# The last step of windowed attention: a sequence's y split one step sooner, y's low parts on GpSimd, and the tail's values ahead of the next gated column

## The chip, the cores and the metric

One core of a Trainium2 chip runs the whole kernel. The metric is the device time of one execution in microseconds (us), lower being better; where several runs are given, their median counts. The engines are TensorE (PE, matmuls; PEld is its weight load), VectorE (DVE), ScalarE (ACT), GpSimd (POOL) and SyncE (SP, which issues most transfers). Each runs its own instructions strictly in order and waits for the others by semaphores.

## The reference

An encoder layer: RMS norm, one input projection, two parallel branches, a gated merge, and a squared-ReLU MLP, for two sequences of 512 tokens and a model width of 1024. The two branches are what the change lies between:

```
y_att = windowed_attention(q, k, v, sink, bias, mask)      # 16 heads of 64, 4 key heads, blocks of 128
y_ssm = s5_branch(u, ...)                                  # ends: y = gelu(scan(u)); y * sigmoid(y @ w_glu + b_glu)
mixed = sigmoid(g_att) * y_att + sigmoid(g_ssm) * y_ssm
x     = x + mixed @ w_out
```

A query block of 128 tokens sees its own key block and the two beside it; a per-head sink logit joins the softmax. All matrices are float32.

## The kernel before, in words

**Precision.** TensorE multiplies in a rounded float32 (`fp32r`). A float32 operand is split: its high part is a cast to `fp32r`, its low part the original minus the high part, again `fp32r`. A product is three matmuls: high by high, low by high, high by low. A split so costs a cast on one engine and a subtraction on another for each 128x512 tile.

**Attention** runs as eight steps `(j, sq)`: four key heads, two sequences each. A step has four query blocks `qb`; a block is a `Unit`, and its work is spread over two passes of the loop. In pass `qb` the current unit computes the scores of its four query heads (`scores`, L1070, into `sps`), adds the bias and finds the maximum (`largest`, L1074, DVE), and takes the exponent (`exp`, L1080, ACT). In the next pass, as `prev`, its probabilities are turned by the identity (`turn`, L1086, four transposes, for each of the two or three key blocks), split into `ph` (L1090, ACT) and `pl` (L1095, DVE), and multiplied with the values (`value`, L1102, into `po`); then ACT copies one half of `po` (`lower_part`, L1106) and DVE adds the other to it (`add`, L1112). When a unit is made, GpSimd copies the sink column into its `p` (L1062). When a step is done, a `Divide` inverts the row sums, sends them round through memory as `fac`, and GpSimd multiplies `ya` by them (`multiply`, L1141) before `mix_scr<-ya` is stored (L1142).

In passes of earlier steps the next step's query projection (L731) lies between these pieces and fills TensorE. The last step, `j = 3, sq = 1` (index 7), has no next one. What fills it is the first column of the gated product `y @ w_glu`: `first_column(k)` (L1204) is six matmuls for one 128-row chunk `k` of y, three for each sequence, summed in two banks over eight chunks, 48 in all. Column 1 follows, dense, as `ahead.multiply` (L769) behind the tail.

**y's split.** Eight chunks `m`, two sequences: sixteen casts (`y_high`, L1189) and sixteen subtractions (`y_low`, L1195 and L1197). All casts are on ACT, both sequences of a chunk as a pair; the subtraction is DVE's for the first sequence and GpSimd's for the second. All lie in the last step, in pass `qb` chunks `2 qb` and `2 qb + 1`. The raw y comes by six transfers on SP (L1184) behind `mix_scr<-ya`; two of the chunks were loaded before the step. The split parts live in two slots of the memory that the normalised input `hT` had used, and which is free once the last projection is done.

**The tail** behind the loop adds what is owed, turns the last unit's probabilities, multiplies its values, and makes column 1's weights ready: their two loads (`c_raw`, L743) are issued at the end of the last pass, then cast (`c_hi`, L747, ACT) and subtracted (`c_lo`, L748, DVE).

The order of the program is written out by hand: what stands earlier in the code is issued earlier on its engine. Transfers are issued by SP in the order of the code.

## Time and profile before

| | |
|---|---|
| three runs | 1461.7, 1463.05, 1465.93 us (median 1463.05) |
| the profiled execution | 1463.26 us, span 1461.5 us, granted clock 0.996 |
| busy in the span | PE 98%, PEld 84%, DVE 75%, ACT 53%, POOL 11% |
| the last step | 635.43 to 664.27 us of the span |
| the tail, to the 31st matmul of column 1 | 664.27 to 675.70 us |

The profile shows one execution. A timeline row gives the start and the length of an instruction (us from the span's start), its engine, its line, the tiles that it writes and reads, its shape, and in brackets how long the engine stood idle before it and what ended that. Matmul rows overlap: the distance between two starts is the time that one takes in a row of them. The windows view gives the busy time of every engine in a stretch.

### The profile page before, as it was taken

The page shows a single profiled execution, that of the slowest core. Times are in us where ns is not written, and L with a number is a line of the kernel's source. Part 1 is how long each engine was busy: PE and PEld are TensorE (multiplying, and loading weights), DVE is VectorE, ACT ScalarE, POOL GpSimd, SP SyncE. Part 2 cuts the span into 40 slices and gives each one's busy share as a digit, 9 for nine tenths or more (in the row PEclk, how much of TensorE's full clock was granted, in tenths as well). Part 3 has the DMA queues.
Part 4 walks back from the last instruction along what each step waited for, and adds up shares of the span by engine and source line. Part 5 has one row for each costly group of instructions (what it writes and reads, how often), then busy time and mean ns, then how long its engine had stood idle before and what let it go on. Part 6 is the DMA issues. An engine that isn't in the chain of part 4 may idle for free.

```text
span 1461.5 us, 21454 instructions
## 1 busy us (share of the span) xinstructions
PE 1436.7 (98%) x7718; PEld 1227.3 (84%) x7718; DVE 1097.0 (75%) x1856; ACT 775.5 (53%) x1398; POOL 168.0 (11%) x250
## 2 busy tenths in 40 slices
PE   7999999999999999999999989999999999999998
PEld 5888888888999999977888868888888888888887
DVE  8799979974536999998954797777776588475653
ACT  5489862133427999896532455455455444333332
POOL 4111120000213444232001000000000000000000
PEclk9999999999999999999999999999999999999999
DMA  8355567259931332358952334444443894454441
GB/s 305 109 172 173 160 203 274 101 173 296 302 95 51 103 107 76 95 170 265 306 182 87 130 110 155 144 153 151 147 151 130 309 352 130 158 187 147 128 130 58
DMA packets 129238, 243.86 MB, mean 167 GB/s; under 512 B 16059, under 2 KB 59323, under 8 KB 129132
## 3 DMA queue, kind: packets, MB, share of 16 engines
q1 hardware_dynamic: 104684, 186.87, 40.4%
q10 hardware_dynamic: 21888, 46.15, 8.4%
q0 software_dynamic: 2560, 9.48, 2.0%
q8 instruction: 61, 1.00, 0.3%
q14 instruction: 45, 0.37, 0.1%
HBM read 173.20 MB, written 81.82 MB: 174 GB/s over the span
## 4 chain that ended last, share of the span: by engine, by line
PE 91%; DVE 3%; DMA 2%; ACT 2%; issue 1%; POOL 1%; SPq 0%; ACTq 0%; DVEq 0%; POOLq 0%
PE bank L115 14%; PE bank L116 14%; PE bank L117 14%; PE acc L141 11%; PE acc L731 9%; PE acc L769 5%; PE acc L115 3%; PE acc L117 3%; PE acc L116 3%; PE po L1102 2%; PE sps L604 2%; PE sps L1070 2%; PE sps L876 2%; PE tps L1086 2%; PE lag L619 1%
## 5 line engine op out<-in xcount | busy, mean ns | idle before, releaser
L116 PE MATMUL bank<-b_lo,a_hi 128*128 128x512 f32 x440 | 171.2, 389 | 0.0
L117 PE MATMUL bank<-b_hi,a_lo 128*128 128x512 f32 x440 | 171.2, 389 | 0.0
L115 PE MATMUL bank<-b_hi,a_hi 128*128 128x512 f32 x440 | 171.2, 389 | 0.0
L731 PE MATMUL acc<-w_hi,hT 128*128 128x256 f32 x768 | 164.9, 291 | 0.0
L141 PE MATMUL acc<-hT,c_hi 128*128 128x512 f32 x512 | 161.2, 394 | 0.0
L1969 ACT CAST a_hi<-d_a 128x1024 fp32r<-128x1024 f32 x55 | 57.9, 1053 | 178.4 <-PE bank L116 175.3
L1970 DVE TENSOR_TENSOR a_lo<-d_a,a_hi 128x1024 fp32r<-128x1024 f32 x55 | 67.4, 1225 | 100.6 <-ACT a_hi L1969 98.5
L731 PEld LDWEIGHTS acc<-w_hi,hT 128*128 128x128 f32 x768 | 126.6, 190 | 1.7
L141 PEld LDWEIGHTS acc<-hT,c_hi 128*128 128x128 f32 x512 | 94.6, 188 | 21.0 <-issue 2.5
L731 PE MATMUL acc<-w_lo,hT 128*128 128x256 f32 x384 | 108.0, 281 | 0.0
L115 PE MATMUL bank<-act,u_hi 128*128 128x512 f32 x256 | 100.7, 393 | 4.7 <-ACT u L1729 4.7
L116 PE MATMUL bank<-act,u_hi 128*128 128x512 f32 x256 | 100.5, 393 | 0.0
L117 PE MATMUL bank<-act,u_lo 128*128 128x512 f32 x256 | 100.3, 392 | 0.0
L141 PE MATMUL acc<-hT,c_lo 128*128 128x512 f32 x256 | 100.3, 392 | 0.0
L117 PEld LDWEIGHTS bank<-b_hi,a_lo 128*128 128x128 f32 x440 | 82.6, 188 | 17.2
L115 PEld LDWEIGHTS bank<-b_hi,a_hi 128*128 128x128 f32 x440 | 82.6, 188 | 17.2
L116 PEld LDWEIGHTS bank<-b_lo,a_hi 128*128 128x128 f32 x440 | 82.6, 188 | 17.1
L1080 ACT ACTIVATE p<-p,nmx 128x257 f32<-128x257 f32 (+1 forms) x128 | 72.0, 564 | 12.9 <-DVE nmx L1074 12.2
L1753 ACT CAST u_hi<-s 128x512 fp32r<-128x512 f32 x64 | 39.9, 623 | 70.1 <-PE bank L116 52.6
L731 PEld LDWEIGHTS acc<-w_lo,hT 128*128 128x128 f32 x384 | 73.0, 190 | 2.5
L1074 DVE CUSTOM_DVE_ANT_0 p<-sps,bias,nsink 128x256 f32<-128x256 f32 (+1 forms) x128 | 69.3, 542 | 3.7 <-PE sps L1070 2.3
L1970 DVE TENSOR_TENSOR b_lo<-k,b_hi 128x1024 fp32r<-128x1024 f32 x55 | 67.1, 1220 | 0.0
(387 smaller groups left out, 3615.6 us busy)
## 6 DMA issues: line engine op xcount, KB each, us to landing
d_a<-a_scr SPq DMA_DIRECT2D x55, 512.0 KB, 3.6
u_raw<-in_w_up_dram SPq DMA_DIRECT2D x32, 512.0 KB, 5.2
a_scr<-t ACTq DMA_DIRECT2D x64, 256.0 KB, 2.1
k<-in_w_down_dram SPq DMA_DIRECT2D x32, 512.0 KB, 5.8
a_scr<-a ACTq DMA_DIRECT2D x48, 256.0 KB, 3.2
c_raw<-in_w_ug_dram SPq DMA_DIRECT2D x44, 256.0 KB, 3.3
ct_scr<-ctab SPq DMA_DIRECT2D x16, 576.0 KB, 3.3
ctab_in<-ct_scr SPq DMA_DIRECT2D x32, 288.0 KB, 4.7
```

The costliest lines, as they stand in the source:

```text
L115: PE.matmul(ps, a[0], b[0], start=first, stop=False)
L116: PE.matmul(ps, a[0], b[1], start=False, stop=False)
L117: PE.matmul(ps, a[1], b[0], start=False, stop=last)
L141: PE.matmul(self.ps[s], self.w[p == 2][:, k, :], hT[s][p == 1][:, k, :], start=i % (3 * KT) == 0, stop=i % (3 * KT) == 3 * KT - 1)
L604: PE.matmul(ps[:, i * P:(i + 1) * P], bm[:, ri, g, :], u_sb[:, g, :], start=True, stop=True)
L731: PE.matmul(ps, act[p == 2][:, k, col:col + P], self.w[k // 4][p == 1][:, k % 4, :], start=i == 0, stop=i == 3 * KT - 1)
L769: PE.matmul(self.ps[s], w_g[self.m][p == 2][:, k, :], y_part(s, int(p == 1), k), start=k + p == 0, stop=k == KT - 1 and p == 2)
L1074: V.tensor_tensor_reduce(self.p[:, h, 1:1 + self.nk], self.s[h][:, 0:self.nk], biases[self.j][h][:, b0:b0 + self.nk], -1.0, nsink[:, hh:hh ...
L1080: S.activation(p, p, AF.Exp, bias=self.nmx[:, h:h + 1], scale=-1.0, accum_out=self.sums[:, h, self.qb:self.qb + 1])
L1753: S.copy(hi, src)
L1969: S.copy(hi, src)
L1970: V.tensor_sub(lo, src, hi.bitcast(F32))
```

## The change

The memory slot for the first sequence's y is opened at the very start, and `hT` of the first sequence lives in it: that `hT` is last read in step 5, so the slot is free for y in step 6. There, in passes 2 and 3, GpSimd casts and subtracts the first sequence's chunks 0 and 1, ahead of `made.multiply`. In the last step ACT makes eight casts instead of sixteen, one at a time (the second sequence's chunks 0 and 1, the first sequence's chunks 2 to 7), DVE six (the second sequence's chunks 2 to 7), and GpSimd all fourteen subtractions. The first two chunks of the first sequence are multiplied in pass 0 right behind the first turn. The gate multiply of step 6's result moves behind the last subtractions. The loads of column 1's weights are issued in the last step right behind y's. In the tail, `first_column(7)` is cut in two around the second turn, the values come ahead of column 1, and column 1's casts and subtractions follow `ph` and `pl`.

```diff
+    slot_a = opers.enter_context(tc.tile_pool(name="slot_a", bufs=1, side="right", reuse_waits="tile"))
-    hT = [[hpool.tile([P, KT, HALF], F32R, name=f"hT{s}_{i}") for i in range(2)] for s in range(NSEQ)]
+    hT = [slot(slot_a), [hpool.tile([P, KT, HALF], F32R, name=f"hT1_{i}") for i in range(2)]]
...
-        def y_high(m, yr):
-            for s in range(NSEQ):
-                S.copy(y_part(s, 0, m).rearrange("p (t k) -> p t k", t=T), yr[:, :, s, :])
-
-        def y_low(m, yr):
-            for s in range(NSEQ):
-                lo, hi = [y_part(s, i, m).rearrange("p (t k) -> p t k", t=T) for i in (1, 0)]
-                if s:
-                    GP.tensor_tensor(lo, yr[:, :, s, :], hi.bitcast(F32), op=ALU.subtract)
-                else:
-                    V.tensor_sub(lo, yr[:, :, s, :], hi.bitcast(F32))
-
-        def first_column(k):
-            for s in range(NSEQ):
+        def y_high(m, s, copy):
+            copy(y_part(s, 0, m).rearrange("p (t k) -> p t k", t=T), y_rows[m][:, :, s, :])
+
+        def y_low(m, s):
+            lo, hi = [y_part(s, i, m).rearrange("p (t k) -> p t k", t=T) for i in (1, 0)]
+            GP.tensor_tensor(lo, y_rows[m][:, :, s, :], hi.bitcast(F32), op=ALU.subtract)
+
+        def first_column(k, seqs=range(NSEQ)):
+            for s in seqs:
...
-                    if i == len(steps) - 1:
-                        y_high(2 * qb, y_rows[2 * qb])
                     cur.scores(1)
...
+                    if last and qb == 1:
+                        w_g[1], parts1 = column_parts(1, False)
+                        for load, part in parts1:
+                            load()
+                    if last and qb:
+                        y_high(2 * qb, 1, V.tensor_copy)
+                        for s in range(NSEQ):
+                            y_low(2 * qb, s)
                     if n3:
                         prev.turn(0)
                         prev.high(0)
+                    if last and not qb:
+                        y_high(0, 1, S.copy)
+                        y_low(0, 1)
                     project(8)
                     if n3:
                         prev.low(0)
-                    if i == len(steps) - 1 and qb:
-                        first_column(2 * qb - 1)
+                    if last:
+                        if qb == 0:
+                            first_column(0, (0,))
+                            first_column(1, (0,))
+                        elif qb == 1:
+                            first_column(1, (1,))
+                        else:
+                            first_column(2 * qb - 1)
...
-                    if made and qb == NB - 1:
+                    if i == len(steps) - 2 and qb >= 2:
+                        y_high(qb - 2, 0, GP.tensor_copy)
+                        y_low(qb - 2, 0)
+                    if made and qb == NB - 1 and not last:
                         made.multiply()
                         made = None
...
-                    if i == len(steps) - 1:
-                        y_low(2 * qb, y_rows[2 * qb])
+                    if last and turned:
+                        turned.low()
+                        turned = None
...
-                    if i == len(steps) - 1:
-                        y_high(2 * qb + 1, y_rows[2 * qb + 1])
+                    if last:
+                        y_high(2 * qb + 1, 0 if qb else 1, S.copy)
...
                     cur.largest(3)
+                    if last:
+                        if qb:
+                            y_high(2 * qb + 1, 1, V.tensor_copy)
+                            y_low(2 * qb + 1, 0)
+                        y_low(2 * qb + 1, 1)
+                        if made and qb == NB - 1:
+                            made.multiply()
+                            made = None
...
-                    if i == len(steps) - 1:
-                        y_low(2 * qb + 1, y_rows[2 * qb + 1])
-                        first_column(2 * qb)
+                    if last:
+                        first_column(2 * qb, range(NSEQ) if qb else (1,))
...
+                    if last and qb < NB - 1:
+                        y_high(2 * qb + 2, 0, S.copy)
                     if n3:
                         prev.lower_part()
...
-                    if i == len(steps) - 1 and qb == NB - 1:
-                        w_g[1], subs_g = column_parts(1)
-                        for sub in subs_g:
-                            sub()
...
-            first_column(KT - 1)
+            first_column(KT - 1, (0,))
             prev.low(0)
             prev.turn(1)
             prev.high(1)
+            first_column(KT - 1, (1,))
+            subs_g = [part() for load, part in parts1]
+            prev.low(1)
+            for sub in subs_g:
+                sub()
+            for n in range(2):
+                for part in range(2):
+                    prev.value(n, part)
+            prev.lower_part()
...
             ahead.multiply(6)
-            prev.value(0, 0)
-            prev.low(1)
+            prev.add()
+            div = Divide(*steps[-1], *done, True)
+            div.invert()
             V.tensor_mul(at0, at0, ga0)
-            prev.value(0, 1)
             ahead.multiply(6)
-            prev.value(1, 0)
+            div.turn()
...
-            ahead.multiply(6)
-            prev.lower_part()
-            prev.add()
-            div = Divide(*steps[-1], *done, True)
-            div.invert()
-            ahead.multiply(12)
-            div.turn()
+            ahead.multiply(18)
             div.multiply()
```

How the instructions stand at three places (the line numbers of the changed kernel are one to a few higher). First TensorE, from the scores that open the last step: `tps<-ident,p` is a turn, `po<-ph,va` a value, and `acc<-act...` the first column. Before:

```order
L1070 MATMUL sps<-kl,qa 128x256
L1086 MATMUL tps<-ident,p 128x128 x4
L1070 MATMUL sps<-kh,qa 128x256
L1070 MATMUL sps<-kl,qa 128x256
L1086 MATMUL tps<-ident,p 128x128 x4
L1102 MATMUL po<-ph,va 128x512
```

and now:

```order
L1071 MATMUL sps<-kl,qa 128x256
L1087 MATMUL tps<-ident,p 128x128 x4
L1200 MATMUL acc<-act_7265,c_hi 128x512
L1200 MATMUL acc<-act_7266,c_hi 128x512
L1200 MATMUL acc<-act_7265,c_lo 128x512
L1200 MATMUL acc<-act_7265,c_hi 128x512
L1200 MATMUL acc<-act_7266,c_hi 128x512
L1200 MATMUL acc<-act_7265,c_lo 128x512
L1071 MATMUL sps<-kh,qa 128x256
L1071 MATMUL sps<-kl,qa 128x256
L1087 MATMUL tps<-ident,p 128x128 x4
L1103 MATMUL po<-ph,va 128x512
```

Six matmuls of the first sequence have come between the first turn and the next scores; before, the first matmul of the column stood behind the second unit of values.

Then ScalarE from the same place (`yr` is a raw chunk of y, `act0` its high part). Before:

```order
L1106 COPY ol_7682<-po_7637 64x512
L1189 CAST act0_7691<-yr_7370 128x512
L1189 CAST act0_7693<-yr_7370 128x512
L1090 CAST ph_7734<-tps_7729 128x512
L1080 ACTIVATE p_7709,sm_7696<-p_7709,nmx_7711 128x257 x2
L1090 CAST ph_7753<-tps_7748 128x512
L1189 CAST act0_7691<-yr_7372 128x512
L1189 CAST act0_7693<-yr_7372 128x512
```

and now:

```order
L1107 COPY ol_7691<-po_7646 64x512
L1091 CAST ph_7736<-tps_7731 128x512
L1189 CAST act0_7697<-yr_7375 128x512
L1081 ACTIVATE p_7713,sm_7700<-p_7713,nmx_7715 128x257 x2
L1091 CAST ph_7764<-tps_7759 128x512
L1189 CAST act0_7697<-yr_7377 128x512
L1081 ACTIVATE p_7713,sm_7700<-p_7713,nmx_7715 128x257
```

The pair of casts that stood ahead of `ph` is gone, and one cast for each chunk stands behind it.

Last GpSimd, from the row statistics of step 6's last pass into the last step (`ya<-ya,fac` is the gate multiply, `p<-nsink` the sink column of a new unit). Before:

```order
L1024 TENSOR_TENSOR rq<-ms,neg_half 128x4
L1141 TENSOR_TENSOR ya<-ya,fac 128x1024
L1062 COPY p<-nsink 128x4
L1023 TENSOR_SCALAR ms<-ms 128x4
L1024 TENSOR_TENSOR rq<-ms,neg_half 128x4
L1195 TENSOR_TENSOR b_7694<-yr,act_7693 128x512 x2
L1062 COPY p<-nsink 128x4
```

and now:

```order
L1025 TENSOR_TENSOR rq<-ms,neg_half 128x4
L1189 CAST act_7265<-yr 128x512
L1193 TENSOR_TENSOR act_7266<-yr,act_7265 128x512
L1142 TENSOR_TENSOR ya<-ya,fac 128x1024
L1063 COPY p<-nsink 128x4
L1024 TENSOR_SCALAR ms<-ms 128x4
L1025 TENSOR_TENSOR rq<-ms,neg_half 128x4
L1193 TENSOR_TENSOR b_7698<-yr,act_7697 128x512 x2
L1063 COPY p<-nsink 128x4
L1193 TENSOR_TENSOR act_7266<-yr,act_7265 128x512
L1193 TENSOR_TENSOR b_7698<-yr,act_7697 128x512
```

A cast and a subtraction of the first sequence have come ahead of the multiply, and from the second pass on each chunk has two subtractions where it had one.

More of the change, by code (lines that the diff above doesn't have):

```diff
@@ L1234, in hybrid_layer @@
                 extra = pieces_of(i)
+                last = i == len(steps) - 1
+                if i == len(steps) - 2:
+                    y_tiles = [[[t_[:, 0:4, :], t_[:, 4:8, :]] for t_ in slot(slot_a)]]
                 if i == len(steps) - 1:
@@ L1357, in hybrid_layer @@
                     hpool_cm.__exit__(None, None, None)
-                    slot_a, slot_b = [opers.enter_context(tc.tile_pool(name=f"slot_{n}", bufs=1, side="right", reuse_waits="tile"))
-                                      for n in "ab"]
-                    y_tiles = [[[t_[:, 0:4, :], t_[:, 4:8, :]] for t_ in slot(slot_a)], split_slot()]
+                    slot_b = opers.enter_context(tc.tile_pool(name="slot_b", bufs=1, side="right", reuse_waits="tile"))
+                    y_tiles.append(split_slot())
             loads_in_order.__exit__(None, None, None)
@@ L1380, in hybrid_layer @@
             ahead.multiply(6)
-            prev.value(0, 0)
-            prev.low(1)
+            prev.add()
+            div = Divide(*steps[-1], *done, True)
+            div.invert()
             V.tensor_mul(at0, at0, ga0)
-            prev.value(0, 1)
             ahead.multiply(6)
-            prev.value(1, 0)
+            div.turn()
             V.tensor_mul(gs0, gs0, y_rows[0])
-            prev.value(1, 1)
             w_g[2], subs_g = column_parts(2)
```

## The prediction

> **What bounds the kernel now.** I read the page's first part, then the stretches of the last attention step, then that stretch's rows engine by engine. On the whole TensorE sets the time:
>
> ```profile
> PE 1436.7 (98%) x7718; PEld 1227.3 (84%) x7718; DVE 1097.0 (75%) x1856; ACT 775.5 (53%) x1398; POOL 168.0 (11%) x250
> ```
>
> So only PE's gaps can be won, and the change touches one place with gaps: the last step (four query blocks, which I call units 0 to 3) and the tail behind it. The windows are those four units, the tail up to the 31st matmul of GLU column 1, and a stretch behind it; columns are length, then busy time and count of PE, PEld, DVE, ACT and POOL:
>
> ```profile
> 635.43:643.41 7.98, 5.75 (x29) 3.87 (x28) 7.14 (x19) 7.16 (x19) 3.91 (x5) 1.00 0.97 351
> 643.41:649.59 6.18, 6.18 (x34) 5.22 (x33) 5.54 (x16) 5.90 (x15) 2.19 (x2) 1.00 0.38 133
> 649.59:657.24 7.65, 7.42 (x40) 5.82 (x38) 7.05 (x17) 7.09 (x18) 3.27 (x5) 1.00 0.83 222
> 657.24:664.27 7.03, 6.87 (x40) 5.43 (x38) 6.41 (x16) 6.28 (x16) 4.96 (x3) 1.00 0.45 145
> 664.27:675.70 11.43, 10.92 (x51) 8.13 (x49) 8.58 (x15) 8.01 (x12) 0.00 (x0) 1.00 0.82 280
> 676.00:690.00 14.00, 14.00 (x63) 11.57 (x62) 13.02 (x16) 7.42 (x12) 1.81 (x3) 1.00 0.95 284
> ```
>
> PE is dense from 676 on, so time won before 675.70 reaches the end undiminished. Idle up to there: 7.98 - 5.75 = 2.23 in unit 0, then 0, 0.23, 0.16 and 0.51: 3.13 us. Clock 1.00 throughout. The gaps by PE's timeline (start, length, in brackets the idle time and what ended it):
>
> ```profile
> 638.30 0.50 PE L1102 MATMUL po<-ph,va 128*128 128x512 f32 x1 [0.94 <-ACT ph L1090]
> ...
> 642.38 0.50 PE L1204 MATMUL acc<-act,c_hi 128*128 128x512 f32 x1 [1.28 <-DVE qa L1050]
> ...
> 644.11 0.60 PE L1086 MATMUL tps<-ident,p 128*128 128x128 f32 x4
> ...
> 657.72 0.60 PE L1086 MATMUL tps<-ident,p 128*128 128x128 f32 x4
> 658.07 0.71 PE L1204 MATMUL acc<-act,c_hi 128*128 128x512 f32 x2
> ...
> 674.31 0.39 PE L769 MATMUL acc<-act,c_hi 128*128 128x512 f32 x1
> ...
> 675.44 0.39 PE L769 MATMUL acc<-act,c_lo 128*128 128x512 f32 x1
> ```
>
> Spacings back to back: a 512-column matmul 0.226 ((675.44 - 674.31)/5); the four scores that open a unit 0.48 at 256 columns (657.72 - 657.24), 0.70 at 384 (644.11 - 643.41); a turn of four transposes 0.35 (658.07 - 657.72). Behind the gap of unit 0 stand ACT's y casts, in the tail GLU column 1's weights, which land late:
>
> ```profile
> 636.50 1.14 ACT L1189 CAST act<-yr 128x512 fp32r<-128x512 f32 x2
> 637.66 0.58 ACT L1090 CAST ph<-tps 128x512 fp32r<-128x512 f32 x1
> ...
> 639.61 1.14 ACT L1189 CAST act<-yr 128x512 fp32r<-128x512 f32 x2
> ...
> 665.79 1.32 ACT L747 CAST c_hi<-c_raw 128x512 fp32r<-128x512 f32 x2 [0.74 <-DMA c_raw<-in_w_glu_dram]
> ```
>
> VectorE's rows of the same stretch: two low parts of y, column 1's subtractions, and the add that frees the value bank.
>
> ```profile
> 639.62 0.69 DVE L1197 TENSOR_TENSOR act<-yr,act 128x512 fp32r<-128x512 f32 x1
> ...
> 660.72 1.38 DVE L1197 TENSOR_TENSOR act<-yr_pair,act 128x512 fp32r<-128x512 f32 x1
> ...
> 666.50 1.33 DVE L748 TENSOR_TENSOR c_lo<-c_raw,c_hi 128x512 fp32r<-128x512 f32 x2 [2.03 <-ACT c_hi L747]
> 667.75 0.84 DVE L1112 TENSOR_TENSOR ya<-po,ol 64x256 f32<-64x256 f32 x2
> ```
>
> **The change, part by part.** PE, ACT and DVE run in order, so I placed the new order unit by unit. "Lead" is how much sooner PE has done the same work.
>
> Unit 0. The two casts ahead of ph go: ph starts 637.66 - 636.50 = 1.16 sooner. Of the pair at 639.61 one stays: 0.57 less ahead of qa, the operand that ended the 1.28 gap. DVE's subtraction at 639.62 goes; its 0.6 was partly covered by qa's wait for ACT, I count half. Together 1.16 + 0.57 + 0.3 = 2.0: unit 1 starts at 641.4 instead of 643.41. Three more column matmuls (first sequence, chunk 1) are done by then, 3 x 0.226 = 0.68. Lead 2.7.
>
> Unit 1 gives back. It was dense before because the gap let ACT and DVE catch up. Now ACT, with 7.16 - 0.57 = 6.6 of work from 635.43, is still 0.65 behind at 641.4. DVE gets a cast ahead of the first pl, and meets POOL. The cast's price is not in the trace: no dense one-source DVE operation of 128x512 with both sides in SBUF exists before. Its bounds:
>
> ```profile
> L337 DVE TENSOR_TENSOR dt<-ex_q,ex_i 128x64 f32<-128x64 f32 x1 | 0.2, 227 | 0.0
> L326 DVE TENSOR_SCALAR ex_n<-ex_r 128x64 f32<-128x64 f32 x2 | 0.4, 196 | 0.1
> L864 DVE COPY st<-h 64x512 f32<-64x512 f32 x32 | 24.3, 767 | 3.6 <-PE sps L876 2.9
> ```
>
> One source saves 0.031 at 64 elements; if that is per element, 0.25 at 512: 0.69 - 0.25 = 0.44, the low end. The high end is the widely strided copy, 0.77. The y cast reads runs of adjacent elements, nearer to the dense rows: I take 0.44. The Trainium skill (VectorE: DVE Perf Modes, § The perf-mode tier table) gives a one-source fp32 copy in SBUF twice the rate of a two-source one, which scaled is an estimate of 0.43; by it the sum is the same, and no row here shows it at this size. While POOL subtracts, a DVE operation waits: the subtraction at 660.72 took 1.38 instead of 0.69 beside the first row here, and the second pair, early in the program, is worse:
>
> ```profile
> 660.25 1.29 POOL L1195 TENSOR_TENSOR b<-yr_pair,act 128x512 fp32r<-128x512 f32 x1
> ```
>
> Of the second pair, VectorE's row and GpSimd's:
>
> ```profile
> 15.37 1.77 DVE L220 TENSOR_TENSOR c_lo<-c_raw,c_hi 128x512 fp32r<-128x512 f32 x1
> ```
>
> ```profile
> 14.98 1.61 POOL L366 TENSOR_TENSOR hT<-rn_xn,hT 128x512 fp32r<-128x512 f32 x1 [3.52 <-ACT hT L364]
> ```
>
> So a blocked operation costs 0.69 to 1.08 more, one that meets nothing 0. By my placing the first cast of a unit comes up late in a POOL subtraction: 0.45. Unit 1 loses 0.65 + 0.44 + 0.45 = 1.5; lead at unit 2: 1.2. Bounds: lead 0 if everything is given back, 2.7 if PE stays dense.
>
> Unit 2: 0.44 + 0.45 less the 0.6 of the subtraction that leaves: loses 0.3, lead 0.9. Unit 3: the same 0.3, 0.3 more because the second cast waits longer (about 0.7), less the 0.69 that 660.72 had waited: gains 0.1. The tail starts 1.0 sooner, at 663.25.
>
> POOL's room: four subtractions and a small copy in each of units 1 to 3, 4 x 1.29 + 0.2 = 5.4 of about 7; in the last also the gate multiply, behind them, whose transfer is not due before the tail is over.
>
> ```profile
> L1062 POOL COPY p<-nsink 128x4 f32<-128x4 f32 x32 | 6.1, 192 | 0.0
> ```
>
> That copy brings in the sink column, which the unit's first exp on ACT reads, and it now stands behind the last subtraction of the unit before. That subtraction needs a DVE cast that follows the unit's last score row: in unit 1 I place it at 648.4, its end at 649.7, the copy's at 649.9 and unit 2's exp at 650.0. Cost nothing, with 0.1 to spare; every further delay on POOL is a delay of exp, up to 1.29 if the subtraction before it is late too. The Trainium skill (GPSIMD Engine Reference, § 4.1) speaks against the move: two-input elementwise work takes about twice as long there as on VectorE. The trace agrees, 1.29 against 0.69; by it the change costs POOL 8 x 1.29 more for 8 x 0.69 saved on DVE, and the sum is unchanged while POOL has room.
>
> Tail. Column 1's weights are now asked for in unit 1 instead of here, so the casts and subtractions at 665.79 and 666.50 no longer wait for a landing; the add (667.75) moves ahead of the subtractions, which frees the bank for the values:
>
> ```profile
> 660.74 1.98 SPq L743 DMA_DIRECT2D c_raw<-in_w_glu_dram  x2
> ```
>
> After 663.25: turn 0.35, three matmuls 0.68, turn 0.35, three matmuls 0.68, to 665.3; the values follow ph and pl (0.58 and 0.69 each, the last pl at about 666.3), and column 1 runs dense from 666.7. Before, 30 back-to-back matmuls ending at 675.70 would start at 675.70 - 30 x 0.226 = 668.9. Lead 2.1.
>
> Step before. Two POOL casts and two subtractions come in ahead. The price of one cast from a copy, then the rows of POOL, of DVE and of PE that the casts meet:
>
> ```profile
> L988 POOL COPY kd<-kn 128x512 f32<-128x512 f32 x8 | 4.9, 610 | 0.0
> ```
>
> ```profile
> 623.42 1.04 POOL L1024 TENSOR_TENSOR rq<-ms,neg_half 128x4 f32<-128x4 f32 x1
> ...
> 631.51 2.41 POOL L1141 TENSOR_TENSOR ya<-ya,fac 128x1024 f32<-128x1024 f32 x1
> ```
>
> ```profile
> 625.81 0.69 DVE L748 TENSOR_TENSOR c_lo<-c_raw,c_hi 128x512 fp32r<-128x512 f32 x1
> ...
> 627.55 0.69 DVE L1095 TENSOR_TENSOR pl<-tps,ph 128x512 fp32r<-128x512 f32 x1
> ```
>
> ```profile
> 628.29 0.50 PE L1102 MATMUL po<-pl,va 128*128 128x512 f32 x1
> ```
>
> The first pair runs 624.4 (623.42 + 1.04) to 626.3 and holds up the subtraction at 625.81: it would end at 626.83 instead of 626.50. DVE has next to no gap from there to the pl at 627.55, whose end at 628.24 is what lets PE's value start at 628.29: -0.33 (0 if the chain has slack, -0.7 as at 660.72). The second pair pushes the multiply, and the stores and loads behind it on SP's queue, by 0.61 + 1.29 = 1.9:
>
> ```profile
> 633.95 0.38 SPq L1142 DMA_DIRECT2D mix_scr<-ya  x1
> 634.42 2.88 SPq L1184 DMA_DIRECT2D yr<-y_scr  x4
> ```
>
> ```profile
> DMA to landing us min/median/max: 5.2/5.7/6.9
> ```
>
> The first load, y block 2, now issues at 636.3 and lands near 641.7 (5.4 later, between the row's least and median); ACT comes to its cast at about 642.0. It is hidden with 0.3 to spare.
>
> Sum: 2.1 - 0.33 = 1.7 us. The profiled execution took 1463.26 with a span of 1461.5 (1.8 around it); the runs' median is 1463.05, 0.2 below. Forecast 1463.05 - 1.7 = 1461.4. A cast of 0.77 takes another 0.33 in each of units 1 to 3, 1.0 in all: 1462.4.
>
> **The rivals.** (B) PE stays bound. Work to 675.70: 102 matmuls (48 of column 0, 24 values, 30 of column 1) x 0.226 = 23.1, scores 0.48 x 4 + 0.70 x 4 = 4.7 (units 0 and 3 have the short ones), 12 turns x 0.35 = 4.2, 0.4 of small transposes: 32.4 of 40.3 us. All idle (3.1) and half of the other 4.8 gone, less 0.33: gain 5.2, 1457.9. For: ACT has eight casts fewer and DVE two operations fewer, and neither is full in the windows. Against: unit 1 was dense only behind 2.23 of idle in unit 0.
>
> (C) Slower: GpSimd's 14 subtractions and DVE's six casts take turns. POOL is busy 5.4 of 7 in units 1 to 3, so a cast meets a running subtraction most times, and each wait is handed on to the sink copy and exp. At 0.69 to 1.08 for each of six instead of the 1.5 that I counted, 4.1 to 6.5: 2.6 to 5.0 more, 3.8 in the middle; a sixth of it I put beside other waits, 3.2 on the path. 1.5 more than the 1.7 gained: 1464.6. It decides once the six casts wait over 1.5 + 1.7 = 3.2 in sum, 0.53 each. The rows above speak for it, most pl and score rows, which read PSUM, at 0.69 and 0.48 to 0.62 against. The Trainium skill (SBUF — State Buffer, § Who interferes with whom) states it as an exclusive lock, the later one blocked for the whole instruction; the trace agrees at 660.72.
>
> (D) The late y loads: block 2 takes the row's longest landing, 6.9 instead of 5.4, and comes at 643.2, 1.2 us after ACT wants it. ACT's casts, the chain behind and unit 1 slip by that: gain 0.5, 1462.5.
>
> (E) No effect: the first stall of unit 0 moves whole to ph and pl in unit 1, and the tail's 1.1 goes to waits of the values and to the step before: 1463.1. For: unit 1's backlog of 0.65. Against: the late landing at 665.79 goes in any case.
>
> **How the numbers follow.** Forecast 0.42, B 0.18, C 0.17, D 0.12, E 0.11. A difference over 0.3% (4.4 us) is what a measurement of this kernel can tell from none. Faster by more needs under 1458.7: two thirds of B, 0.12. Slower by more needs over 1467.4: a fifth of C and 0.03 for what I have not seen, 0.06. Within: 0.82. Range: B's end to C's, 1458.0 to 1465.0.
>
> **What would show it.** Right: PE's 0.94 and 1.28 gaps of unit 0 gone or under half; unit 1 longer than PE's content; DVE casts of 0.4 to 0.5 where POOL rests, 0.9 to 1.2 where not; no wait for c_raw in the tail; dense column 1 about 2 us sooner against the step's start, and the step's own start 0.3 later. Wrong: PE waiting for act parts from POOL, ACT's exp waiting for POOL, ACT waiting for yr, DVE casts of 1.2 and more throughout, or PE idle under 1 us in the whole stretch.

## The result, and the profile after

The changed kernel takes 1456.25 us (median of nine runs, 1454.72 to 1459.61), the kernel before 1463.45 us beside it (nine runs, 1461.7 to 1466.78): a ratio of 0.9950, 95% interval 0.9937 to 0.9963. It is 7.2 us faster; the forecast was 1.7 us, and the time lies below the range. The profiled execution took 1455.62 us with a span of 1453.8.

The change's own stretch came out near the forecast in size. The gain has another source, 180 us behind it, at a place that the prediction does not mention.

**The last step.** The page's busy times after the change, for the whole span:

```profile
PE 1434.8 (99%) x7718; PEld 1227.8 (84%) x7718; DVE 1094.3 (75%) x1854; ACT 770.0 (53%) x1390; POOL 179.3 (12%) x260
```

The windows of the four units, of the tail up to the 31st matmul of column 1, and of two stretches behind it, after the change (length; busy time and count of PE, PEld, DVE, ACT, POOL; granted clock; DMA share; GB/s):

```profile
635.90:641.92 6.02, 5.43 (x32) 4.46 (x31) 5.87 (x17) 5.55 (x15) 4.53 (x7) 1.00 0.74 214
641.92:648.76 6.84, 6.32 (x31) 4.63 (x30) 5.68 (x16) 5.24 (x14) 3.87 (x3) 1.00 1.03 411
648.76:656.69 7.93, 7.57 (x39) 5.84 (x38) 6.57 (x18) 6.89 (x17) 6.17 (x6) 1.00 0.74 231
656.69:663.68 6.99, 6.71 (x40) 5.51 (x39) 5.80 (x15) 4.85 (x13) 5.24 (x6) 1.00 0.23 58
663.68:674.16 10.48, 10.48 (x50) 8.20 (x49) 7.79 (x13) 8.60 (x14) 3.30 (x3) 1.00 0.67 219
674.00:690.00 16.00, 16.00 (x72) 13.15 (x71) 14.97 (x17) 6.54 (x11) 4.55 (x4) 1.00 1.02 354
690.00:703.00 13.00, 11.57 (x52) 9.22 (x51) 11.61 (x15) 5.97 (x10) 0.00 (x0) 1.00 0.90 291
```

Counted from the start of the step, units 1, 2, 3 and the tail begin at 6.02, 12.86, 20.79 and 27.78 us; before, at 7.98, 14.16, 21.81 and 28.84. So the lead is 1.96, 1.30, 1.02 and 1.06, where 2.0, 1.2, 0.9 and 1.0 was forecast. The 31st matmul of column 1 is reached 10.48 behind the tail's start instead of 11.43, a lead of 2.0 (forecast 2.1); with the later start of the step (635.90 against 635.43) 1.54 us are left at 674.16 (forecast 1.7).

The last row but one is dense; the last has 1.43 us of idle, and before it had none. That is the first place where the forecast breaks: the waits of PE between 690 and 712, after the change (the time in all, the count, the longest; before, this stretch has none):

```profile
PE acc L770 <- DVE c_lo L749: 1.4, 1, 1.4
```

The operand that column 4 starts with comes from DVE's subtraction, which starts almost when it did before. The row of the changed kernel, then of the kernel before, by DVE's timeline:

```profile
701.38 1.29 DVE L749 TENSOR_TENSOR c_lo<-c_raw,c_hi 128x512 fp32r<-128x512 f32 x2
```

```profile
701.54 1.28 DVE L748 TENSOR_TENSOR c_lo<-c_raw,c_hi 128x512 fp32r<-128x512 f32 x2
```

Only 0.16 sooner. With the matmuls of the two traces paired by their number, the lead is 1.6 at 670, and 0.12 to 0.16 from 704 to 850. All that the edits won was gone 30 us behind them.

**Where the 7 us come from.** At 851 the output projection ends and the up projection of the MLP begins. Of the kernel before, the waits of PE have this row, the longest of the program behind its first products:

```profile
PE bank L115 <- ACT u L1729: 4.7, 1, 4.7
```

PE's timeline of the kernel before, the last matmul into the old accumulators, the first into the new ones, and the thirteenth:

```profile
851.10 0.39 PE L117 MATMUL acc<-act,f 128*128 128x512 f32 x1
856.23 0.79 PE L115 MATMUL bank<-act,u_hi 128*128 128x512 f32 x1 [4.74 <-ACT u L1729]
...
861.35 0.40 PE L115 MATMUL bank<-act,u_hi 128*128 128x512 f32 x1
```

Its windows of the idle time and of those twelve matmuls:

```profile
851.00:856.20 5.20, 0.49 (x3) 0.07 (x1) 5.11 (x10) 4.52 (x8) 0.00 (x0) 0.82 0.02 9
856.23:861.09 4.86, 4.86 (x12) 3.80 (x12) 4.78 (x8) 3.60 (x6) 0.00 (x0) 0.50 0.17 53
```

PE stands idle for 4.74 us, and then runs at a granted clock of 0.50: twelve matmuls in 5.1 us (856.23 to 861.35), 0.426 each instead of 0.227. After the change the same place reads, by PE's timeline:

```profile
850.94 0.39 PE L117 MATMUL acc<-act,f 128*128 128x512 f32 x1
851.17 0.39 PE L115 MATMUL bank<-act,u_hi 128*128 128x512 f32 x1
```

No wait, and no slow matmuls: 4.74 + 12 x (0.426 - 0.227) = 7.1 us. The paired matmuls show 7.3, a lead of 0.16 at 850 and 7.47 at 863, which stays to the end; the 0.16 between the two is there because the idle time is counted from the end of a row of 0.39, in a stream whose rows start 0.227 apart.

**Why the wait was there.** The front of the program has three accumulators, handed out again as they come free; the up projection opens a new pool of eight over the same memory. Behind 851 ACT still has to copy one old accumulator out, and comes to it late, since its other work is queued ahead (ACT's timeline, before):

```profile
854.56 0.63 ACT L1741 ACTIVATE a<-a 128x512 f32<-128x512 f32 x1
...
855.59 0.59 ACT L1729 COPY u<-acc 128x512 f32<-128x512 f32 x1 [0.40 <-ACT a L1741]
```

In the program's assignment of memory that accumulator lies, before the change, on the same bank (bank 0) as the first of the eight new ones. In the changed kernel `first_column` asks for its first accumulator earlier, ahead of the one that the query turn of the step uses; the two change places, and from there on banks 0 and 2 are swapped for every later accumulator of the front. The one that ACT copies late is then on bank 2, which the up projection needs later.

### The profile page after: what moved, and what is told of

Its sections match the earlier page's. It is cut to its first block, busy times and chain, and to the rows that moved or that the text cites. A ratio compares the mean times of both kernels' runs of the same rounds, so it can differ in the third digit from the quotient of the medians.

```text
span 1453.8 us, 21452 instructions
## 1 busy us (share of the span) xinstructions
PE 1434.8 (99%) x7718; PEld 1227.8 (84%) x7718; DVE 1094.3 (75%) x1854; ACT 770.0 (53%) x1390; POOL 179.3 (12%) x260
## 4 chain that ended last, share of the span: by engine, by line
PE 90%; DVE 4%; DMA 2%; ACT 1%; issue 1%; POOL 0%; SPq 0%; DVEq 0%; ACTq 0%
PE bank L116 14%; PE bank L117 14%; PE bank L115 14%; PE acc L141 11%; PE acc L732 9%; PE acc L115 3%; PE acc L117 3%; PE acc L116 3%; PE acc L770 3%; PE po L1103 2%; PE sps L605 2%; PE sps L1071 2%; PE sps L877 2%; PE tps L1087 2%; PE lag L620 1%
## 5 line engine op out<-in xcount | busy, mean ns | idle before, releaser
L732 PE MATMUL acc<-w_hi,hT 128*128 128x256 f32 x384 | 84.4, 293 | 0.0
L732 PE MATMUL acc<-w_hi,act 128*128 128x256 f32 x384 | 81.2, 290 | 0.0
L141 PE MATMUL acc<-act,c_hi 128*128 128x512 f32 x256 | 80.6, 395 | 0.0
L141 PE MATMUL acc<-hT,c_hi 128*128 128x512 f32 x256 | 80.5, 394 | 0.0
L732 PEld LDWEIGHTS acc<-w_hi,hT 128*128 128x128 f32 x384 | 63.8, 190 | 0.9
L732 PEld LDWEIGHTS acc<-w_hi,act 128*128 128x128 f32 x384 | 63.1, 190 | 0.8
L1993 ACT CAST b_hi<-k 128x1024 fp32r<-128x1024 f32 x55 | 57.7, 1051 | 0.0
```

Of the source, the lines that this page charges most:

```text
L141: PE.matmul(self.ps[s], self.w[p == 2][:, k, :], hT[s][p == 1][:, k, :], start=i % (3 * KT) == 0, stop=i % (3 * KT) == 3 * KT - 1)
L732: PE.matmul(ps, act[p == 2][:, k, col:col + P], self.w[k // 4][p == 1][:, k % 4, :], start=i == 0, stop=i == 3 * KT - 1)
L1993: S.copy(hi, src)
```

## The experiments

Two theories for the gain. **Rotation:** the swap of the accumulators, and nothing else, makes the 7 us; the edits of the last step are worth nothing in the end. **Edits:** the changed last step makes at least a good part of it. For the slow matmuls: the halved clock follows from the idle time. For the lost lead: several causes of the late operand, below.

**1. Only the rotation, in the kernel before.** One dummy transpose takes an accumulator more in the output projection, so that all later ones move on by one place; nothing of the change is in it.

```diff
             add = rows1[t].half(1)
+            if t == 3:
+                PE.transpose(acc()[:, 0:P], ident, ident)
             if t == 3:
```

> The kernel before with one small transpose more (0.1 us) into an accumulator late in the output projection, so that the three accumulators rotate on by one and the first product of the up projection no longer falls on the accumulator that ACT copies as u; attention is untouched. Theory 1 (the measured gain comes from this collision, 180 us behind the change): no 4.7 us wait at the up projection, no spell at half clock behind it, 1463.4 - 7.3 = 1456.1. Theory 2 (the gain comes from the attention step, as the change meant): 1463.4, no change.

Measured: 1456.12 us, ratio 0.9947 (0.9932 to 0.9961). PE's timeline at the place has no idle time any more:

```profile
850.48 0.39 PE L115 MATMUL bank<-act,u_hi 128*128 128x512 f32 x1
```

One line that computes nothing gives the whole gain of the change.

**2. The collision put back into the changed kernel.** The same line, there.

> The changed kernel with the same small transpose, which there turns the accumulators so that the collision is back; the attention step stays changed. Theory 1: the wait of 4.7 us for ACT's u and the half clock are back, 1456.3 + 7.3 = 1463.6, level with the kernel before. Theory 2: 1456.3, the gain stays.

Measured: 1462.89 us, ratio 0.9996 (0.9988 to 1.0005). PE's timeline and the window of what follows the idle time:

```profile
856.57 0.80 PE L115 MATMUL bank<-act,u_hi 128*128 128x512 f32 x1 [4.74 <-ACT u L1755]
```

```profile
856.57:861.20 4.63, 4.63 (x11) 3.71 (x12) 4.54 (x8) 3.60 (x6) 0.00 (x0) 0.50 0.13 46
```

The wait and the half clock are back, and with them the time of the kernel before. This is also the measure of the edits alone, with the dummy transpose of 0.1: between 1.8 us faster and 0.7 us slower by the interval. Rotation holds, edits falls.

**3. The idle time filled, in the kernel before.** Twenty more matmuls of the same shape into a spare tile keep PE busy until ACT's copy is done; the collision stays.

```diff
     p1 = product(acc(), first[1][0], B11)
     p2 = product(acc(), first[1][1], B21)
+    fill = tps()
+    for _ in range(20):
+        PE.matmul(fill, first[1][1][0][:, 0, :], B21[0][:, 0, :], start=True, stop=True)
```

> The kernel before with 20 extra matmuls of 128x512 (4.5 us, result unused) in the gap ahead of the up projection, so that TensorE does not idle while it waits for ACT's u. Theory A (the twelve slow matmuls at 0.43 us are the price of the idle stretch, through the granted clock): the first product still starts near 856.2, the matmuls behind it take 0.227, 2.4 us less: 1461.0. Rival B (the first products are slow by what they read or by what runs beside them): 1463.4, still 0.43 each.

Measured: 1461.51 us, ratio 0.9985 (0.9976 to 0.9993). PE's timeline, and the window of what follows:

```profile
856.28 0.50 PE L115 MATMUL bank<-act,u_hi 128*128 128x512 f32 x1 [0.22 <-ACT u L1729]
```

```profile
856.30:861.00 4.70, 4.70 (x21) 3.90 (x22) 4.61 (x8) 3.89 (x7) 0.00 (x0) 1.00 0.13 45
```

Full clock, and the up projection starts when it did. So the slow matmuls come from the idle time ahead of them, and not from what runs beside them. 2.4 us were expected of it and 1.6 came; the lead by paired matmuls is 2.2 at 863 and 1.7 at the end, and the 0.5 lost between 1200 and 1300 were not followed.

**4. Half filled:** nine matmuls instead of twenty, one run.

> The kernel before with 9 extra matmuls (2.0 us) at the start of the gap ahead of the up projection, so that 2.7 us of idle are left of 4.9. If any idle of this length halves the granted clock, the twelve slow matmuls stay; if the clock falls only after a longer idle, they run at 0.227 as with 20. I expect the latter, with no rule of this case to say so.

Measured: 1462.23 us (one run; 1463.25 before on the same chip). PE's timeline:

```profile
855.85 0.50 PE L115 MATMUL bank<-act,u_hi 128*128 128x512 f32 x1 [2.70 <-ACT u L1729]
...
856.90 0.54 PE L116 MATMUL bank<-act,u_hi 128*128 128x512 f32 x1
857.24 0.63 PE L117 MATMUL bank<-act,u_lo 128*128 128x512 f32 x1
```

Against what was expected, 2.70 us of idle time also halve the clock, but not at once: behind the first, three matmuls follow at about 0.23, and from 856.90 on they take up to 0.43 until 860.2, some 3.3 us.

The next runs ask why the lead of 1.6 us is lost at column 4.

**5. The subtractions of the next column's weights put ahead of the mixing** in each column of the changed kernel.

```diff
                 gl = bank_out(m, col.ps[s])
-                if not ending:
-                    low = late()
                 for sub in subs:
                     sub()
+                if not ending:
+                    low = late()
```

> The changed kernel with one move in the gated columns: the subtractions that make the next column's low weights stand ahead of the mixing of the column before on VectorE, not behind it. Theory 1 (the attention step did win 1.8 us, and 1.4 of it are lost again where TensorE waits for c_lo at the fourth column): that wait goes, 1456.3 - 1.4 = 1454.9. Rival (VectorE is full there, and what is now late takes the wait's place): 1456.3.

Measured: 1455.59 us, ratio 0.9943 (0.9930 to 0.9955), and the wait for `c_lo` is still 1.4. The time lies between the two answers expected; by the wait, this order in DVE's queue is not what holds the operand: in the trace the gate product ahead of it now waits 1.91 for `ga`, and the subtraction starts at 701.18.

**6. GpSimd's last gate multiply left out**, in the changed kernel; the values that it scales go out unscaled, so a part of the attention's result is missing. It runs from 685.75 and holds up a DVE operation that takes 0.69 elsewhere (DVE's timeline of the changed kernel):

```profile
686.24 2.61 DVE L1580 TENSOR_TENSOR at<-z,at 128x512 f32<-128x512 f32 x1
```

```diff
             ahead.multiply(18)
-            div.multiply()
+            GP.dma_start(mix_scr[6:8, :, HALF:2 * HALF].rearrange("m p t -> p m t"), div.ya)
```

> The changed kernel without GpSimd's last gate multiply (128x1024, 2.4 us; left out, so the last key head's second sequence is stored unscaled). Theory 1 (the 1.4 us lost at the fourth column come from this multiply, which blocks a VectorE operation for 1.9 us at 686 and so delays the gate product, the load of the next gate and at last c_lo): no VectorE row of 2.6, the wait for the gate's load (1.28) gone or small, no wait for c_lo, 1456.2 - 1.4 = 1454.8. Rival (VectorE is paced by the gate's load in any case): c_lo where it was, 1456.2.

Measured: 1455.33 us, ratio 0.9947 (0.9934 to 0.9961); the wait is 0.9. Without the blocked operation the gate products of DVE still stand at 689.98 and 695.83, now waiting for `w_raw` (1.36) and `ga` (0.98). The wait is 0.5 shorter in this one trace, with PE 0.3 later; in the median the difference is no larger than the runs' scatter. What the change did move is where the block falls: GpSimd's multiply ran at 691.52 in the kernel before, behind the gate product of 688.73; now it runs at 685.75, ahead of that product, which stands at 689.98. That this is what costs the lead is not shown, since the product stands there without the multiply too.

**7. The gate product put ahead of the mixing**, so that its buffer comes free, and its next load starts, sooner (changed kernel; `gate_at` is the product of `at` and `ga`, taken out of `gate_in`). The subtractions stand ahead of the mixing too, as in run 5.

```diff
-            V.tensor_mul(at, at, ga)
...
-                if not ending:
-                    low = late()
                 for sub in subs:
                     sub()
...
+                if gate:
+                    gate_at(gate)
+                if not ending:
+                    low = late()
                 if gate:
                     gate_in(gate, low)
```

> The changed kernel with another order on VectorE in the gated columns: first the next column's low weights, then the product with the gate, which frees the gate's buffer, and only then the mixing of the column before. Theory 1 (the gate's load is issued late because its buffer is freed late): the load is issued some 1.5 us sooner at the third column, the idle time of 1.28 goes, c_lo at the fourth column is 1 to 1.5 us sooner and so is all that follows: 1455.0. Rival (the column stage is bound by VectorE's sum of work, the order does nothing): 1456.2.

Measured: 1461.23 us, ratio 0.9984 (0.9975 to 0.9993): 5 us worse than the changed kernel, and neither of the answers expected. The waits of PE, and a window behind them:

```profile
PE acc L770 <- ACT c_hi L748: 2.4, 1, 2.4
PE acc L770 <- DVE c_lo L749: 0.6, 1, 0.6
```

```profile
704.00:708.00 4.00, 3.89 (x9) 3.12 (x10) 3.28 (x6) 1.21 (x2) 0.00 (x0) 0.50 0.85 282
```

DVE waits for `ga` with the mixing queued behind it, ACT's cast comes late in turn, and the idle time of 3.0 us brings the half clock here too.

**8. The tail and the early weights alone**, in the kernel before (one run): column 1's loads in unit 1, the tail in its new order, y's split as it was.

```diff
+                    if i == len(steps) - 1 and qb == 1:
+                        w_g[1], parts1 = column_parts(1, False)
+                        for load, part in parts1:
+                            load()
...
-            first_column(KT - 1)
+            first_column(KT - 1, (0,))
...
+            first_column(KT - 1, (1,))
+            subs_g = [part() for load, part in parts1]
+            prev.low(1)
...
```

> The kernel before with only the tail of the change: column 1's weights loaded behind y, the last values and the last add ahead of column 1; y's split stays as it was. Theory 1 (by my sum the tail is worth 1.1 us, the rest of the 2.2 comes from the moved casts): from the step's start at 635.4 to the 31st matmul of column 1 39.2 us instead of 40.3, then all of it lost at the fourth column; total level with before. Rival (late weights were the whole local gain): 38.0 us.

Measured: 1467.8 us, one run, against 1463.25; level was expected. The waits:

```profile
PE bank L115 <- ACT u L1731: 4.7, 1, 4.7
PE acc L769 <- DVE c_lo L748: 1.8, 1, 1.8
```

From the step's start the 31st matmul of column 1 comes after 39.32 us, as expected (39.2; 40.27 in the trace before). But runs 1 and 4, which leave the last step as it was, reach it after 39.37 and 39.34 (more on this below). This trace begins the step 0.75 later than the one before, so by paired matmuls it leads by only 0.25 at 670; through the wait at column 4 and the slow clock behind it, it is 3.0 behind from 706 on. The collision is still there: the early request for an accumulator in pass 0 belongs to y's split, not to the tail.

**9. The store that SP waits for.** In the changed kernel `mix_scr<-ya` goes out at 666.41, behind the moved gate multiply (664.00 to 666.4), and the loads behind it with it; the DMA engines stand still from 660 to 664. Here that multiply is left out and its store issued earlier (the mixing of that part takes values without their gate).

```diff
+                    if made and qb == NB - 1 and last:
+                        SP.dma_start(mix_scr[2 * made.j:2 * made.j + 2, :, made.sq * HALF:(made.sq + 1) * HALF].rearrange("m p t -> p m t"), made.ya)
+                        made = None
...
-                            made.multiply()
```

> The changed kernel without GpSimd's gate multiply of the seventh result (step 6) in the last step; its store to mix_scr goes out on SP in the same step without it, so the mixing takes an ungated value there (that part of the output is left out). Theory: in the changed kernel the store at 666.41 waits behind that multiply (664.00 to 666.4), and every load behind it on SP with it, so that the DMA engines stand idle until 664 to 668 and the fourth column waits 1.4 us for c_lo. Without the multiply the store is issued before 664, the engines are busy from about 660 on, the wait for c_lo falls under .5, and the end comes 1.0 to 1.6 sooner: 1454.9. Rival: the gate loads are paced by their buffers and by the transfers of the weights, the wait stays over 1.0 and the time is that of the changed kernel, 1456.2.

Measured: 1457.34 us, ratio 0.9958 (0.9945 to 0.9970), beside 1456.48 for the changed kernel itself on the same chip (ratio 0.9959, 0.9946 to 0.9971):

> The changed kernel itself, as the measure for the two others: 1456.2, as in its first runs, with a wait of the fourth column for c_lo of 1.4 us and no wait of the up projection's first product.

The wait for `c_lo` is 1.8, not under 0.5. SP's queue without the multiply, then with it:

```profile
656.93 0.32 SPq L1560 DMA_DIRECT2D gs<-gs_scr  x1
666.93 0.94 SPq L744 DMA_DIRECT2D c_raw<-in_w_glu_dram  x2
```

```profile
666.41 0.38 SPq L1143 DMA_DIRECT2D mix_scr<-ya  x1
...
667.39 1.33 SPq L744 DMA_DIRECT2D c_raw<-in_w_glu_dram  x2
```

The theory falls. SP is free ten microseconds earlier, and still issues column 2's weights at 666.93: their two buffers hold column 1's weights until DVE has subtracted them (from 666.22 on). Before the change it was 667.22, with DVE's subtraction from 666.50 on. So behind these loads nothing starts sooner here.

**10. The same multiply in the middle:** between the two pairs of low parts of the last pass.

```diff
+                        if made and qb == NB - 1:
+                            made.multiply()
+                            made = None
...
-                        if made and qb == NB - 1:
-                            made.multiply()
-                            made = None
```

> The changed kernel with GpSimd's gate multiply of the seventh result between the two pairs of low parts instead of behind them. Theory: its store leaves SP's queue about 3 us sooner, the wait of the fourth column for c_lo falls by about 1 us, while the second pair of low parts comes later by the multiply's 2.4 us, of which the matmuls of the last step see at most .3: 1455.3. Rival: the low parts behind the multiply come too late for the unit that reads them and the last step loses what the store wins: 1456.2 or more, up to 1458 if all 2.4 us show.

Measured: 1456.16 us, ratio 0.9959 (0.9945 to 0.9972): no difference to the changed kernel's 1456.48. The store goes out at 662.66, but column 2's weights at 667.63; the wait for `c_lo` is 1.2.

**11. The buffers freed sooner:** as 10, and column 1's casts and subtractions at the end of unit 3.

```diff
                     if n3:
                         prev.lower_part()
+                    if last and qb == NB - 1:
+                        for load, part in parts1:
+                            part()()
...
-            subs_g = [part() for load, part in parts1]
+            subs_g = []
```

> The kernel with the gate multiply in the middle, and besides with column 1's two casts and two subtractions at the end of unit 3 instead of in the tail. Theory after e12_nomul6: the loads of column 2's weights are issued at 667 in every kernel so far because their two buffers are freed by column 1's subtractions (666.2 to 667.9); all that stands behind them on SP's queue, and the column 4 operand at 701.3, hangs on that. With the subtractions about 3 us earlier those loads are issued at about 664, the fourth column's wait for c_lo falls from 1.2 to under .4, and the time is about 1455.2. Rival: the transfers behind are paced by later buffers (column 3's weights at 688 to 689, the gate tiles), the wait stays at 1.0 or more, and the casts in unit 3 delay the last units by .3 to .6: 1456.5.

Measured: 1459.41 us, ratio 0.9965 (0.9951 to 0.9978): slower than both answers expected. The waits of PE:

```profile
PE acc L770 <- DVE c_lo L749: 2.8, 1, 2.8
PE po L1103 <- DVE pl L1096: 1.0, 2, 0.8
PE po L1103 <- DVE ya L1113: 1.1, 1, 1.1
```

The subtractions came only 1.4 us sooner (665.23), the loads at 665.95; the values of the tail now wait behind them, 1.9 us more (0.8 + 1.1), and column 4's operand is later still, 2.8, with the clock at 0.79 and 0.78 in the two windows behind. So freeing the buffers in this way does not pay, and whether they alone hold column 4 stays open.

What stays open: in runs 6, 9 and 10 and in the changed kernel the gate product ahead of column 4's operand starts at 695.83 to 696.13, each time behind 0.98 to 1.91 us of waiting for `ga`, and 5.2 us of DVE's work lie between it and the operand. `ga` has one buffer: in the changed kernel its load is issued at 691.22, as soon as the gate product of 689.98 (1.21 long) has read it, and in the kernel before at 689.98, behind the product of 688.73. The DMA share is 0.94 to 1.07 from 668 to 696. DVE's row of the changed kernel:

```profile
696.13 1.23 DVE L1566 TENSOR_TENSOR at<-at,ga 128x1024 f32<-128x1024 f32 x1 [1.28 <-DMA ga<-ga_scr]
```

So the buffer sets when the load starts; what its landing owes to the full DMA engines was not separated, and a second buffer for `ga` was not tried. A caution on runs 5 to 10: column 4's subtraction starts at 701.38, 701.46 and 701.88 in three traces of the same changed code up to there (its own, its repeat beside run 9, and run 2), and at 700.68 to 701.55 in four of the old (the kernel before and runs 1, 3 and 4). A few tenths between single traces therefore say nothing about a cause.

## Why the prediction was wrong

**What held.** The local sizes, against the one trace before: unit 1 starts 1.96 sooner (2.0), unit 2 1.30 (1.2), unit 3 1.02 (0.9), the tail's lead is 2.0 (2.1), the sum at 674 is 1.54 (1.7). The gap of 1.28 at `qa` is 0.59 and that of 0.94 is gone. PE's and DVE's rows after the change:

```profile
640.86 0.50 PE L1200 MATMUL acc<-act,c_hi 128*128 128x512 f32 x1 [0.59 <-DVE qa L1051]
```

```profile
645.01 0.42 DVE L1189 CAST act<-yr 128x512 fp32r<-128x512 f32 x1
...
654.83 0.87 DVE L1189 CAST act<-yr 128x512 fp32r<-128x512 f32 x1
...
661.56 1.13 DVE L1189 CAST act<-yr_pair 128x512 fp32r<-128x512 f32 x1
```

The cast, of which no row existed, takes 0.42 (taken as 0.44; the copy that was the high end, 0.77, is ruled out). GpSimd blocks it, by 0.45 and 0.71, but it is the second cast of units 2 and 3 that meets a subtraction, not the first of each unit as placed: the casts at 645.01, 652.22 and 658.83 are clean, and so is the second of unit 1 (648.82, 0.42). Unit 1 therefore never paid the 0.45 counted in it, and gave back 1.34 all the same (forecast 1.5); that this comes so near is in part luck, and what took the rest was not followed.

**The tail, by luck.** The 1.1 that the tail was to add rests on weights that land late in the trace before, where ACT's cast waits 0.74 for them. In run 1, whose last step is that of the kernel before, ACT's row shows no such wait:

```profile
664.62 1.14 ACT L747 CAST c_hi<-c_raw 128x512 fp32r<-128x512 f32 x2
```

There, and in run 4, the tail takes 10.55 and 10.51 us to the 31st matmul of column 1; in the changed kernel it takes 10.48. So of the local lead 0.95 is a late landing that two of four executions of the old step do not have, and the new order of the tail adds next to nothing beyond it.

**The step before.** The term of 0.33 held in its place and was too small by 0.1. In all nine executions with this part of the change, the value matmul at 628.29 of the trace before slips by 0.43 to 0.45 against the matmuls just ahead of it, and 0.40 to 0.44 is left at the step's start; the four executions of the old step 6 in runs 1, 3, 4 and 8 slip by 0.01 at most. Of the 0.47 between 635.43 and 635.90 this execution was 0.07 late already before.

**First failing step:** "PE is dense from 676 on, so time won before 675.70 reaches the end undiminished." Dense says only that PE's work was not waiting then; it does not say how much earlier the operands could have been there. They came just in time: when PE is 1.6 us earlier, column 4's operand is not, and 1.4 of the 1.6 us turned into a new wait. The old step shows the same without any of the edits: runs 1 and 4 are 1.2 and 1.5 ahead of the trace before at 700, wait 0.3 and 1.1 for `c_lo`, and keep 0.8 and 0.35. What holds the operand stays open: runs 5, 6, 9, 10 and 11 each take away one thing ahead of it, and none gets it more than 0.3 us sooner.

**Second failing step:** "only PE's gaps can be won, and the change touches one place with gaps". The largest gap behind the opening, 4.74 us with another 2.4 of half clock behind it, was in the trace before, 180 us further on, and the ranking of PE's waits over the whole program shows it in its second row. It hung on which accumulator came first, and the change asks for accumulators in another order. Runs 1 and 2 show this in both directions: 7.0 us from the rotation alone, and none of it left once the rotation is put back. Sum as it should have been: 0.1 that outlasts column 4, and 7.3. That the kernel became faster, as forecast, is luck.

**The rivals.** B gave 1457.9, near the time but not by its mechanism: the local gain of 5.2 did not come. C needed more than 3.2 us of waits of the six casts; they waited 1.16. D, the late y block, would have made 0.5 of the 1.7; 1.54 was there at 674, and ACT's casts wait for no y in the trace after. E, no effect, comes closest for the edits themselves (run 2: ratio 0.9996), though what ate the gain was column 4, not unit 1. None had a term outside the stretch that the change names.

## What to carry to other kernels

Before costing a change, rank the waits of the bounding engine over the whole program, and ask of each large one whose buffer it waits for: an edit that only alters the order in which a shared pool is asked can move such a wait, far from where it stands. A dummy request that turns the rotation by one place tests it with one line, in both directions. And a dense stretch behind the change is no proof that the gain passes through: look at the slack of the operands that arrive there. And take the trace before more than once: a wait that one execution shows, as for column 1's weights, can be absent from the next.

## What the runs showed of the hardware

The granted clock falls after idle time on TensorE, and the time lost to it comes on top of the wait: 4.74 us of idle time were followed by about 5 us at 0.50, twelve matmuls at 0.426, and 2.70 us by about 3.3 us (run 4). The waits alone do not order what follows: one of 1.8 us in run 8 brought the half clock, and one of 1.8 in run 9 did not. How the idle time lies does: in all traces here the times between two changes of the granted clock are whole multiples of 3.41 us, and the idle time within one such stretch goes with the clock of the next. Windows on these stretches, two each of run 4, run 8 and run 9:

```profile
853.59:857.00 3.41, 1.15 (x5) 0.96 (x6) 3.32 (x6) 2.94 (x6) 0.00 (x0) 1.00 0.23 82
857.00:860.41 3.41, 3.41 (x10) 2.64 (x9) 3.41 (x7) 2.59 (x6) 0.00 (x0) 0.50 0.00 0
```

```profile
701.59:705.00 3.41, 1.65 (x8) 1.06 (x7) 3.38 (x6) 1.21 (x2) 0.00 (x0) 1.00 0.84 257
705.00:708.41 3.41, 3.41 (x10) 2.64 (x9) 3.38 (x5) 1.75 (x3) 0.00 (x0) 0.50 0.89 323
```

```profile
698.29:701.71 3.42, 1.85 (x9) 1.20 (x7) 3.39 (x5) 0.34 (x1) 0.00 (x0) 1.00 0.77 275
701.71:705.12 3.41, 3.13 (x14) 2.56 (x15) 3.38 (x6) 1.00 (x3) 0.00 (x0) 1.00 0.78 246
```

PE idles 2.26 us in the first stretch of run 4 and 1.76 in that of run 8, and the next is at half clock, so that it sets in only behind the gap; the wait of run 9 is cut in two, 1.57 and 0.28, and costs nothing. Behind the first 25 us, every full-clock stretch of these traces with up to 1.57 us of idle time was followed by full clock and every one with 1.95 or more by half; 1.76 (half) and 1.87 (full, at the end of run 8) lie between. The full clock came back after a stretch without idle time; one with 0.62 (run 7, 703.19 to 706.60) kept the half. The Trainium skill (TensorE: Matmul & The Clock Gate, § What's actually happening) puts the fall to half rate at an idle window of about 3.4 us, and the return at about as long a busy one. The rate agrees (0.426 at 512 columns, and 0.50), and so does the length of a slow stretch, 3.41 us or twice that; that 1.76 to 2.7 us are enough does not follow from a whole idle window.

A short filler in such a gap is worth something even where the wait itself can't be shortened: run 3 won 1.6 us with twenty matmuls whose result nobody reads.
